# A fourth seven-product pair in every second group of the last stage's first matrix

## The chip, the cores and the metric

The kernel runs on one core of a Trainium2 chip. Its engines are TensorE (PE in the profile, with PEld for the loading of its stationary operand), VectorE (DVE), ScalarE (ACT), GpSimd (POOL) and SyncE (SP), which issues the transfers. Each engine works through its own queue in order and waits on semaphores of the others. The metric is the device time of one execution in microseconds (us). Each measurement is a median over runs; lower is better.

## The reference, cut to what matters

A decoder trunk of two layers on 256 tokens of width 2048. Layer 0 mixes tokens by retention, layer 1 by a gated convolution; each layer ends in a SwiGLU feed-forward part with 5632 hidden columns. The change lies in the feed-forward part of layer 1, the last stage:

```python
D_MODEL, SEQ, DEPTH = 2048, 256, 2
D_FF = -(-8 * D_MODEL // (3 * 256)) * 256     # 5632

def swiglu(h, w_in, w_out):
    a, b = jnp.split(h @ w_in, 2, axis=-1)
    return (jax.nn.silu(a) * b) @ w_out
...
        h = (rms_norm(x, norm2_g[i]) * (1.0 + sc2) + sh2).astype(x.dtype)
        x = (x + g2 * swiglu(h, ffn_w_in[i], ffn_w_out[i])).astype(x.dtype)
    return rms_norm(x, final_g).astype(x.dtype)
```

`w_in` (2048 x 11264) is the first matrix of the stage, `w_out` (5632 x 2048) the second.

## The kernel before

**Arithmetic.** Every float32 operand is split into a high part (the value rounded to the matmul's input type) and a low part (the rest). A product is three matmuls: high by high, high by low and low by high (`thrice`, L470 to L475). ACT casts the high part of the weights (L408), DVE subtracts it from the weights to get the low part (L411). All weights come from memory in 1 MB blocks of 128 x 2048 (`raw`, three buffers), on SP's queue, in the order of their use.

**Weight places.** The prepared high and low parts lie in rings of six places of 1024 columns each (`PLACES`, L403 to L415). PE takes the places in order (`take`); a place can be written again when PE has used it up.

**The last stage.** The hidden columns are handled in two parts, of 20 and 24 tiles of 128 columns. In each part a stretch of first-matrix work is followed by a stretch of second-matrix work. After eight column tiles done in another form (`first_rows`), the first matrix runs in ten groups, 0 to 3 in the first part and 4 to 9 in the second (`LAST_IN`, `last_input`). A group makes four hidden tiles: two blocks of 512 columns (one of `a`, one of `b`) for two halves of 128 tokens, that is four accumulators (`ours`), summed over the 2048 rows of the weights. These rows come as eight *pairs* (0 to 7) of two 128-row tiles; one pair is one 1 MB block. Second-matrix groups have the same form with other pairs.

**An ordinary pair** (`Group`, `by_token`) has two row tiles, two column blocks and two token halves: eight products, 24 matmuls. Its block is prepared as one piece of 2048 columns, in two places.

**A seven** (`Seven`, `sevens`) does the same pair as a 2 x 2 block product with seven products instead of eight (the Strassen-Winograd form), 21 matmuls. It needs sums of the weight blocks and of the activations. The block is prepared in four pieces, four places: (2) the blocks B22 and B21 as they are, (3) two differences T1 and T3 (L395, in a single buffer, which the profile calls `x`), (4) B11 and T2 (L399), (5) T4 (L401), 512 columns wide. PE uses them in the order B22, B21, T1, T3, B11, T2, T4. Four of the products are gathered in four banks of their own over all sevens of a group. After the last seven of the group `mixed_sums` combines them (L1255 to L1259), and when the group is complete the four accumulators are added (L1330), the gate product is made (L1334, L1335), and its tiles are turned by PE at pair 2 of the next group (`turned`, L1344 to L1351). After this the hidden tiles are split on ACT and DVE (L1348, L1349), and for every second one of some groups sums for the second matrix are made (L1156 to L1159, L525).

**The activations' sums.** `made_in_sums` (L1171 to L1183) makes, once, for each pair that is ever a seven, the four sums s1 to s4 of its four activation blocks, and splits each into high and low. Three go to tiles taken from a list of free ones (`single_sums`), the fourth, s3, overwrites the block of `h` that the seven form doesn't use (a21). A pair with s3 in that place cannot be an ordinary pair later. Pairs 3, 4 and 6 are sevens in all ten groups (`IN_SEVEN`, L41).

**Order.** PE's order is written out in the program; on the other engines a scheduler orders the instructions within their data dependences and priorities when the program is built.

Of the kernel before, what the change touches and what calls it, by code (L numbers as in the profile page):

```python
# [11 lines left out]
F32R = mybir.dt.float32r  # L12
# [5 lines left out]
P = 128  # L18
D = 2048
S = 256  # L20
KT = D // P
# [4 lines left out]
DV = 512  # L26
DFF = 5632
# [10 lines left out]
LEAD = 6  # L38
ROOTS_AT, SPREAD_AT = 1, 3
TAIL_ROWS = 6  # L40
IN_SEVEN, OUT_SEVEN, TURNS_AT, BESIDE_CB, BESIDE_SUMS = (3, 4, 6), ((2, 4, 6), (2, 4, 6)), 2, 40, 48  # L41
LAST_TILES = 20, 24
STORE_AT, LOAD_AT = 0, 2
LEAD_RET, LEAD_CONV, LEAD_FFN = 6, 4, 2
# [97 lines left out]
class Seven:  # L142
# [6 lines left out]
    n = 2 * DV // P  # L149
# [12 lines left out]
def in_pairs(cols, rows, sevens):  # L162

    return [Seven(cols, r) if i in sevens else Group(cols, DV, ks=r) for i, r in rows]


def last_in():

    n, rows = LAST_TILES[0], [(i, [2 * i, 2 * i + 1]) for i in range(KT // 2)]
    cols = [part * DFF + j * P for j in range(n - 4, n) for part in range(2)]
    firsts = [Group(cols[:LEAD])] + [Group([c]) for c in cols[LEAD:]]
    fours = [[*range(0, n - 4, 4)], [*range(n, FT, 4)]]
    return firsts, [[in_pairs([j * P, DFF + j * P], rows, IN_SEVEN) for j in js] for js in fours]


def last_out(part):
# [78 lines left out]
def trunk(ctx: ExitStack, tc: tile.TileContext, x_in, c_in, pos_in, w_mod, cols_in, gain_in, tab_in, w_all, out):  # L257
    nc = tc.nc
    const = ctx.enter_context(tc.tile_pool(name="const", bufs=1))
# [10 lines left out]
    def tmp(tag, shape=(P, S), dtype=F32, pool=work, bufs=None):  # L270
        return pool.tile(list(shape), dtype, tag=tag, name=name(tag), bufs=bufs)
# [10 lines left out]
    n_cols = cols_in.shape[1]  # L282
    cols = const.tile([P, n_cols], F32, tag="cols", name="cols")
# [74 lines left out]
    groups = [g for _, _, g in in_use_order()]  # L358
# [3 lines left out]
    in_seven, n = set(), 0  # L362
# [114 lines left out]
    def half_of(h, t):  # L477
        return [h[:, i, t * P : (t + 1) * P] for i in range(2)]
# [127 lines left out]
    h = rows_at(EARLIER)  # L606
# [85 lines left out]
    with ExitStack() as inner:  # L692
# [372 lines left out]
        h = rows_at(0)  # L1065

    mixing = ctx.enter_context(ExitStack())
    mpool = mixing.enter_context(tc.tile_pool(name="mpool", bufs=1))
# [28 lines left out]
    for i, g in enumerate(CONV_IN):  # L1097
        pending += [sums(g)] if i else normed(acc, 1, 0, g)
        while len(pending) >= 3:
            pb, pc, pu = pending[:3]  # L1100
            pending = pending[3:]
            j = done
# [17 lines left out]
    mpool = ctx.enter_context(tc.tile_pool(name="last", bufs=1))  # L1120
# [3 lines left out]
    h = rows_at(EARLIER)  # L1124
# [25 lines left out]
    single_sums = [in_cb[:, n * P : (n + 2) * P].rearrange("p (i n) -> p i n", i=2) for n in (12, 14)]  # L1150

    def tokens_sums_of(a11, a21, a12, a22, third, others):

        u = tmp("u512", (P, DV), pool=mpool, bufs=3)
        s1, s2, s4, s3 = [u[:, n * P : (n + 1) * P] for n in range(4)]
        nc.vector.tensor_tensor(s3, a11, a21, op=ALU.subtract)  # L1156
        nc.vector.tensor_tensor(s1, a21, a22, op=ALU.add)
        nc.vector.tensor_tensor(s2, s1, a11, op=ALU.subtract)
        nc.vector.tensor_tensor(s4, a12, s2, op=ALU.subtract)  # L1159
        split(third, s3)  # L1160
        n = 3 * P // len(others)
        for i, dst in enumerate(others):
            split(dst, u[:, i * n : (i + 1) * n])

    def parts(both):

        return [both[:, i, t * P : (t + 1) * P] for i in range(2) for t in range(2)]

    in_sums = {}

    def made_in_sums():  # L1171

        tmp("beside_sums", (P, BESIDE_SUMS), bufs=1)
        for tag, n in (("u", 3), ("low", 2), ("sum", 4)):
            single_sums.extend(tmp(tag, (P, 2, P), F32R, bufs=n) for _ in range(n))
        for i in IN_SEVEN:
            both = tmp("u512", (P, 2, S), pool=mpool, bufs=3)
            for n in range(2):
                k = 2 * i + n
                high, low = [h[k].bitcast(F32)[:, v, :] for v in range(2)]  # L1180
                nc.vector.tensor_tensor(both[:, n, :], high, low, op=ALU.add)
            in_sums[i] = [single_sums.pop() for _ in range(3)]
            tokens_sums_of(*parts(both), h[2 * i][:, :, P:], in_sums[i])  # L1183

    def three(v):
        return [v[0][:, :, n * P : (n + 1) * P] for n in range(3)] if len(v) == 1 else v
# [8 lines left out]
    def gate_stored():  # L1195
        needed(1, GT2)
        pt = bank()
        nc.tensor.transpose(pt[:KT, 0, :P], mod_g[1][1], ident)
        row = tmp("row", (KT, P), pool=mpool, bufs=1)
        nc.scalar.copy(row, pt[:KT, 0, :P])  # L1200
        nc.sync.dma_start(gate_row, row)

# [33 lines left out]

    def sevens(g, act, base, sums, ours, banks, first, last):

        s1, s2, s4 = [[v[:, n, :] for n in range(2)] for v in sums]
        (a11, s3), (a12, a22) = [[half_of(act[k - base], t) for t in range(2)] for k in g.ks]  # L1240
        p1, p5, p6, p7 = [(b, first, last) for b in banks]
        for use, x, (o, a, z) in zip(g.uses(), (s4, a12, s1, s3, a11, s2, a22), (
            (ours[0, 1], False, False), (ours[0, 0], False, False), p5, p7, p1, p6, (ours[1, 0], False, False)
        )):
            thrice(o, x, take(*use), a, z)
            if use[2] in ("B21", "T3", "T2"):
                paced(4)
        paced(4)
# [33 lines left out]
    def gathered(groups, act, base, sums, beside=None, mixed=None):  # L1282

        ours = {(t, j): flat_bank() for t in range(2) for j in range(2)}
        banks, n = [], len(sums)
        for i, g in enumerate(groups):
            if beside:
                beside(i)
            if i == TURNS_AT and waiting:
                waiting.pop(0)()  # L1290
            if isinstance(g, Seven):
                n -= 1
                banks = banks or [flat_bank() for _ in range(4)]
                of = sums[(g.ks[0] - base) // 2]
                sevens(g, act, base, of, ours, banks, n == len(sums) - 1, n == 0)
                if not n:
                    extra = mixed_sums(banks)
                    if mixed:
                        mixed(extra)
                continue  # L1300
            if len(g.cols) == 1:
                tail = TAIL_ROWS if g is groups[-1] else 0
                late, j = [], g.cols[0] // DV % 2
                for k in g.ks:
                    weights = take(g, k, *g.items[0])
                    rows = (act[k - base], False, k == g.ks[-1])
                    if tail:
                        late.append((*weights, *rows))
                    else:
                        by_token([ours[t, j] for t in range(2)], *weights, *rows)  # L1310
                    paced(g.n)
                for t in range(2):
                    for args in late:
                        by_token([ours[t, j] for t in range(2)], *args, halves=[t])
                    added(t, g.cols[0] // DV, ours[t, j], True)
                    if tail:
                        stored(t)
                continue
            for k in g.ks:
                for j, item in enumerate(g.items):  # L1320
                    ends = i == 0 and k == g.ks[0], g is groups[-1] and k == g.ks[-1]
                    by_token([ours[t, j] for t in range(2)], *take(g, k, *item), act[k - base], *ends)
                paced(g.n)
        return ours, extra

    def last_input(groups, pairs, seven):

        ours, extra = gathered(groups, h, 0, in_sums)
        for (t, j), pt in ours.items():
            nc.vector.tensor_tensor(extra[t, j], pt, extra[t, j], op=ALU.add)  # L1330
        ms = []
        for t in range(2):
            m = extra[t, 0]
            nc.scalar.activation(m, m, AF.Silu)  # L1334
            nc.vector.tensor_tensor(m, m, extra[t, 1], op=ALU.mult)  # L1335
            ms.append(m)

        def turned():
            for n, (dst, of) in enumerate(zip(pairs, seven)):
                pt = bank()  # L1340
                for i in range(2):
                    for t, m in enumerate(ms):
                        c = slice((2 * n + i) * P, (2 * n + i + 1) * P)
                        nc.tensor.transpose(pt[:, i, t * P : (t + 1) * P], m[:, c], ident)  # L1344
                if of is not None:
                    both = tmp("u512", (P, 2, S), pool=mpool, bufs=3)
                    nc.scalar.copy(both, pt)
                nc.scalar.copy(dst[:, :, 0, :], pt)  # L1348
                nc.vector.tensor_tensor(dst[:, :, 1, :], pt, dst[:, :, 0, :].bitcast(F32), op=ALU.subtract)  # L1349
                if of is not None:  # L1350
                    tokens_sums_of(*parts(both), dst[:, 0, :, P:], of)  # L1351

        waiting.append(turned)
# [47 lines left out]
    for part in range(2):  # L1401
        n = LAST_TILES[part] // 2
# [48 lines left out]
```

## Time and profile before

| | us |
|---|---|
| median of 3 runs | 2594.94 (2594.69 to 2596.77) |
| the profiled execution, its own time | 2595.16 |
| its span, first to last instruction | 2593.4 |
| groups 0 to 3 (first matrix, first part) on PE | 1925.45 to 2094.43 |
| groups 4 to 9 (first matrix, second part) on PE | 2201.28 to 2454.69 |

In the profile, L is a line of the kernel. A timeline row has the start, the duration, the engine, the line, the operation, output and input tiles with their sizes, and the number of instructions merged in the row; in brackets stands how long the engine was idle before, and who released it. Rows of one engine overlap a little, because an instruction starts before the one ahead of it has drained: what an instruction costs a busy engine is the distance between starts. A windows row has the stretch, its length, then for PE, PEld, DVE, ACT and POOL the busy time with the number of instructions, the granted clock of TensorE, the share of the DMA engines and GB/s.

### The profile page before, as it was taken

The numbers are of one execution on the slowest core, as the hardware profiler recorded it, in microseconds if no ns is written. First come the engines' busy times: TensorE is split into PE (matmuls) and PEld (weight loads), VectorE is DVE, ScalarE is ACT, GpSimd is POOL, SyncE is SP. The second block draws the span as 40 slices with busy tenths as digits, with TensorE's granted clock in tenths as the row PEclk, the third lists the DMA queues.
The fourth block names the chain that finished last, engine by engine and source line by source line (L and its number), as shares of the span: only waits on it lengthen the run. The fifth ranks groups of instructions, "written<-read, shape, count | busy, mean of one in ns | idle before, by whom it ended". The sixth has DMA issues, their size and how long they took to land.

```text
span 2593.4 us, 35836 instructions
## 1 busy us (share of the span) xinstructions
PE 2560.4 (99%) x14181; PEld 2236.5 (86%) x14181; DVE 2167.7 (84%) x2378; ACT 1301.9 (50%) x1792; POOL 158.3 (6%) x232
## 2 busy tenths in 40 slices
PE   7999999999999999999999999999999999999998
PEld 6898889888889888888888898888998888888886
DVE  7988878787698887777777889988988988999877
ACT  5544543444456444334454454444565554555554
POOL 0000000200000000111101200000000000000002
PEclk9999999999999999999999999999999999999999
DMA  9975768767676888778777768887845465455553
GB/s 398 386 309 199 275 239 302 296 260 276 245 284 248 314 335 312 278 306 303 291 299 291 288 248 302 329 304 281 307 155 220 179 234 204 177 213 188 218 200 142
DMA packets 96684, 689.53 MB, mean 266 GB/s; under 512 B 10737, under 2 KB 12161, under 8 KB 13441
## 3 DMA queue, kind: packets, MB, share of 16 engines
q1 hardware_dynamic: 96514, 687.23, 70.4%
q8 instruction: 111, 1.82, 0.3%
q14 instruction: 59, 0.48, 0.1%
HBM read 685.08 MB, written 2.11 MB: 265 GB/s over the span
## 4 chain that ended last, share of the span: by engine, by line
PE 93%; DVE 3%; issue 2%; DMA 1%; ACT 1%; ACTq 0%; POOLq 0%; POOL 0%; DVEq 0%
PE bank L460 29%; PE bank L463 15%; PE bank L473 12%; PE bank L474 12%; PE bank L475 12%; PE bank L509 2%; PE bank L508 2%; PE bank L507 2%; PE bank L640 1%; PE bank L642 1%; PE bank L641 1%; DVE lo L411 1%; DVE raw L768 1%; DMA raw<-w_all 1%; PE bank L996 1%
## 5 line engine op out<-in xcount | busy, mean ns | idle before, releaser
L408 ACT CAST hi<-raw 128x1024 fp32r<-128x1024 f32 (+1 forms) x954 | 968.2, 1032 | 900.2 <-DMA raw<-w_all 344.7
L411 DVE TENSOR_TENSOR lo<-raw,hi 128x2048 fp32r<-128x2048 f32 (+2 forms) x570 | 1078.8, 1901 | 257.8 <-ACT hi L408 256.2
L460 PE MATMUL bank<-h,hi 128*128 128x512 f32 x2016 | 699.2, 390 | 0.0
L463 PE MATMUL bank<-h,lo 128*128 128x256 f32 x2016 | 568.4, 282 | 0.0
L460 PEld LDWEIGHTS bank<-h,hi 128*128 128x128 f32 x2016 | 378.3, 188 | 79.2
L318 DVE SCALAR_TENSOR_TENSOR raw<-raw,cb 128x2048 f32<-128x2048 f32 x160 | 365.9, 2287 | 75.8 <-DMA raw<-w_mod 75.8
L473 PE MATMUL bank<-hi,h 128*128 128x512 f32 x1032 | 404.4, 392 | 2.5 <-DVE rm L752 2.5
L474 PE MATMUL bank<-lo,h 128*128 128x512 f32 x1032 | 402.9, 390 | 0.0
L475 PE MATMUL bank<-hi,h 128*128 128x512 f32 x1032 | 402.1, 390 | 0.0
L463 PEld LDWEIGHTS bank<-h,lo 128*128 128x128 f32 x2016 | 381.0, 189 | 0.0
L460 PE MATMUL bank<-mid,hi 128*128 128x512 f32 x922 | 319.8, 390 | 0.0
L463 PE MATMUL bank<-mid,lo 128*128 128x256 f32 x922 | 260.0, 282 | 0.0
L473 PEld LDWEIGHTS bank<-hi,h 128*128 128x128 f32 x1032 | 194.3, 188 | 40.8 <-DVE rm L752 3.2
L475 PEld LDWEIGHTS bank<-hi,h 128*128 128x128 f32 x1032 | 194.0, 188 | 41.0
L474 PEld LDWEIGHTS bank<-lo,h 128*128 128x128 f32 x1032 | 194.2, 188 | 37.5 <-DVE lo L411 0.3
L460 PEld LDWEIGHTS bank<-mid,hi 128*128 128x128 f32 x922 | 173.0, 188 | 36.3
L463 PEld LDWEIGHTS bank<-mid,lo 128*128 128x128 f32 x922 | 174.3, 189 | 0.0
L460 PE MATMUL bank<-rm,hi 128*128 128x512 f32 x496 | 172.5, 390 | 0.0
L509 PE MATMUL bank<-h,lo 128*128 128x256 f32 x512 | 146.7, 286 | 5.5 <-DVE lo L411 5.5
L507 PE MATMUL bank<-h,hi 128*128 128x256 f32 x512 | 146.2, 286 | 3.5 <-ACT h L796 3.5
L508 PE MATMUL bank<-h,hi 128*128 128x256 f32 x512 | 146.1, 285 | 0.7 <-DVE h L797 0.7
L463 PE MATMUL bank<-rm,lo 128*128 128x256 f32 x496 | 139.8, 282 | 0.0
(256 smaller groups left out, 3230.3 us busy)
## 6 DMA issues: line engine op xcount, KB each, us to landing
raw<-w_all SPq DMA_DIRECT2D x456, 1024.0 KB, 4.9
raw<-w_mod SPq DMA_DIRECT2D x192, 1024.0 KB, 5.1
x<-x_in SPq DMA_DIRECT2D x4, 512.0 KB, 5.4
out<-xt SPq DMA_DIRECT2D x4, 512.0 KB, 3.0
decay<-tab_in SPq DMA_DIRECT2D x8, 128.0 KB, 3.4
x<-gate_row SPq DMA_DIRECT2D x2, 512.0 KB, 4.4
last_gain<-gain_in SPq DMA_DIRECT2D x1, 1024.0 KB
cols<-cols_in SPq DMA_DIRECT2D x1, 152.0 KB, 8.9
```

The costliest lines, as they stand in the source:

```text
L318: nc.vector.scalar_tensor_tensor(raw, raw, 1.0, cb, op0=ALU.mult, op1=ALU.mult, accum_out=total)
L408: nc.scalar.copy(hi[:, o], raw[:, o])
L411: nc.vector.tensor_tensor(lo, raw, hi.bitcast(F32), op=ALU.subtract)
L460: nc.tensor.matmul(pt, hi, h, start=fresh and k == g.ks[0], stop=False, skip_group_check=True)
L463: nc.tensor.matmul(pt[:, 1, :], lo, h[:, 0, :], start=False, stop=last and k == g.ks[-1], skip_group_check=True)
L473: nc.tensor.matmul(o, hi, w_hi, start=first, stop=False)
L474: nc.tensor.matmul(o, hi, w_lo, start=False, stop=False)
L475: nc.tensor.matmul(o, lo, w_hi, start=False, stop=last)
L507: nc.tensor.matmul(pt, hi, h[:, 0, :], start=first, stop=False, skip_group_check=True)
L508: nc.tensor.matmul(pt, hi, h[:, 1, :], start=False, stop=False, skip_group_check=True)
L509: nc.tensor.matmul(pt, lo, h[:, 0, :], start=False, stop=last, skip_group_check=True)
L640: nc.tensor.matmul(pt, hi, high, start=k == 0, stop=False, skip_group_check=True)
```

## The change

In groups 0, 2, 4, 6 and 8 of the ten, pair 5 is a seven as well: these groups have the sevens 3, 4, 5 and 6 in a row, the others 3, 4 and 6 as before. Because pair 5 stays an ordinary pair in the other groups, its block a21 of `h` has to stay, and s3 of pair 5 gets a tile of its own (`third`). With its other three sums that makes four tiles; the list of free ones is longer by one, which lies over the tile of the modulation's columns (`cols`), and it is taken from the end, so the sums of the other pairs move by one tile. The tile for the gate's row (`row`) is no longer one of its own, but one of the three `u512` buffers.

```diff
-IN_SEVEN, OUT_SEVEN, TURNS_AT, BESIDE_CB, BESIDE_SUMS = (3, 4, 6), ((2, 4, 6), (2, 4, 6)), 2, 40, 48
+IN_SEVENS, OUT_SEVEN, TURNS_AT, BESIDE_CB, BESIDE_SUMS = ((3, 4, 5, 6), (3, 4, 6)), ((2, 4, 6), (2, 4, 6)), 2, 40, 48
...
     fours = [[*range(0, n - 4, 4)], [*range(n, FT, 4)]]
-    return firsts, [[in_pairs([j * P, DFF + j * P], rows, IN_SEVEN) for j in js] for js in fours]
+    sevens = {j: IN_SEVENS[i % 2] for i, j in enumerate(sum(fours, []))}
+    return firsts, [[in_pairs([j * P, DFF + j * P], rows, sevens[j]) for j in js] for js in fours]
...
-        for i in IN_SEVEN:
+        single_sums.append(const.tile([P, n_cols], F32R, tag="cols", name="in_cols")[:, : 2 * P].rearrange(
+            "p (i n) -> p i n", i=2
+        ))
+        for i in IN_SEVENS[0]:
...
-            tokens_sums_of(*parts(both), h[2 * i][:, :, P:], in_sums[i])
+            third = h[2 * i][:, :, P:]
+            if i not in IN_SEVENS[1]:
+                third = mpool.tile([P, 2, P], F32R, tag="third", name="third")
+                in_sums[i].append(third)
+            tokens_sums_of(*parts(both), third, in_sums[i][:3])
...
-        row = tmp("row", (KT, P), pool=mpool, bufs=1)
+        row = tmp("u512", (P, DV), pool=mpool, bufs=3)[:KT, :P]
...
-        s1, s2, s4 = [[v[:, n, :] for n in range(2)] for v in sums]
+        s1, s2, s4, *third = [[v[:, n, :] for n in range(2)] for v in sums]
         (a11, s3), (a12, a22) = [[half_of(act[k - base], t) for t in range(2)] for k in g.ks]
+        s3 = third[0] if third else s3
...
-        ours, extra = gathered(groups, h, 0, in_sums)
+        used = [g.ks[0] // 2 for g in groups if isinstance(g, Seven)]
+        ours, extra = gathered(groups, h, 0, {i: in_sums[i] for i in used})
```

## The prediction

> **What bounds the kernel now.** I read the page first.
>
> ```profile
> span 2593.4 us, 35836 instructions
> PE 2560.4 (99%) x14181; PEld 2236.5 (86%) x14181; DVE 2167.7 (84%) x2378; ACT 1301.9 (50%) x1792; POOL 158.3 (6%) x232
> PE 93%; DVE 3%; issue 2%; DMA 1%; ACT 1%; ACTq 0%; POOLq 0%; POOL 0%; DVEq 0%
> ```
>
> PE is busy 99% of the span and is 93% of the chain that ended last, so work taken from PE shortens the kernel wherever the others keep up. DVE's 84% is an average; the windows view, cut at the boundaries of the groups that change (in order 0, 2, 4, 6, 8) and, second, of one that does not, says how it stands where the change is.
>
> ```profile
> 1925.45:1967.24 41.79, 41.79 (x187) 34.36 (x185) 39.38 (x59) 25.43 (x40) 0.00 (x0) 1.00 0.53 197
> 1967.24:2009.62 42.38, 42.38 (x192) 35.17 (x191) 38.08 (x39) 24.09 (x27) 0.00 (x0) 1.00 0.54 199
> 2009.62:2052.01 42.39, 42.39 (x192) 35.17 (x191) 39.26 (x45) 25.24 (x30) 0.00 (x0) 1.00 0.55 198
> 2201.28:2242.76 41.48, 41.48 (x185) 34.35 (x183) 37.73 (x39) 21.95 (x23) 0.00 (x0) 1.00 0.54 197
> 2285.15:2327.53 42.38, 42.38 (x192) 35.17 (x191) 39.42 (x45) 25.22 (x30) 0.00 (x0) 1.00 0.53 197
> 2369.92:2412.31 42.39, 42.39 (x193) 35.17 (x192) 39.25 (x45) 25.18 (x30) 0.00 (x0) 1.00 0.53 200
> ```
>
> After the length come PE, PEld, DVE, ACT and POOL, each with its count. PE never waits for long, at full granted clock (1.00), but in group 2 DVE has only 42.39 - 39.26 = 3.13 us left. What a seven costs each engine decides.
>
> **PE's gain.** Ordinary pairs take 24 matmuls and a seven 21, so each of the five groups loses three. The price is the distance of starts, not the duration. Here are the first matmuls of pairs 4 and 5 of group 2; pair 4 is a seven.
>
> ```profile
> 2031.61 0.39 PE L473 MATMUL bank<-hi,low 128*128 128x512 f32 x1
> 2036.37 0.39 PE L473 MATMUL bank<-hi,h 128*128 128x512 f32 x1
> ```
>
> 21 matmuls in 4.76 us are 0.2267 us each. 3 x 0.2267 = 0.68 us a group, 3.4 us in all: 0.13% of the time if nothing else moves. By the duration that the rows show (0.39 us each) it would be 15 x 0.39 = 5.85 us. The Trainium skill's "Perfetto Trace Analysis" (Identifying the Most-Contended Engine) says matmul busy share is a poor measure because matmuls are pipelined; the two starts above bear that out, 0.23 apart against 0.39 long.
>
> **DVE's cost of a seven.** DVE rows of group 2, from the turned tiles of the group before to the end of pair 4. The order of the changed program is the same up to the last row, which there begins pair 5.
>
> ```profile
> 2013.88 2.29 DVE L411 TENSOR_TENSOR lo<-raw,hi 128x2048 fp32r<-128x2048 f32 x1
> 2016.08 1.22 DVE L395 TENSOR_TENSOR x<-raw 128x1024 f32<-128x1024 f32 x1
> ...
> 2022.25 0.69 DVE L1349 TENSOR_TENSOR mid<-bank,mid 128x512 fp32r<-128x512 f32 x1 [0.34 <-ACT mid L1348]
> ...
> 2025.07 1.22 DVE L395 TENSOR_TENSOR x<-raw 128x1024 f32<-128x1024 f32 x1
> 2026.20 0.55 DVE L525 TENSOR_TENSOR in_cb<-u,in_cb 128x384 fp32r<-128x384 f32 x1
> 2026.67 1.22 DVE L411 TENSOR_TENSOR lo<-raw,hi 128x1024 fp32r<-128x1024 f32 x1
> 2027.81 0.68 DVE L399 TENSOR_TENSOR raw<-raw,x 128x512 f32<-128x512 f32 x1
> 2028.41 1.22 DVE L411 TENSOR_TENSOR lo<-x,hi 128x1024 fp32r<-128x1024 f32 x1
> 2029.55 0.68 DVE L401 TENSOR_TENSOR raw<-raw 128x512 f32<-128x512 f32 x1
> 2030.15 1.82 DVE L411 TENSOR_TENSOR lo<-raw,hi 128x1024 fp32r<-128x1024 f32 x2
> 2031.88 1.22 DVE L395 TENSOR_TENSOR x<-raw 128x1024 f32<-128x1024 f32 x1
> ```
>
> An ordinary pair is one 2048-wide subtraction, start to start 2016.08 - 2013.88 = 2.20 us. A seven is seven DVE instructions, 2031.88 - 2025.07 = 6.81 us less the 0.47 of L525 between them: 6.34 us. Start to start, a 1024-wide one is 1.14, a 512-wide one 0.60. So pair 5 adds 4.14 us to DVE and takes 0.68 from PE. In groups 2, 6 and 8 DVE's work becomes about 39.3 + 4.1 = 43.4 us against 42.39 - 0.68 = 41.7 for PE. Worse, pairs 3 to 6 stand in one block, where DVE needs 6.34 a pair and PE 4.76, and the six places of prepared halves hold one and a half sevens (four places each): DVE cannot build up a lead in the groups between, and L1349 above waits for ACT's copy of what PE turns at pair 2 of the same group, so DVE cannot run ahead of that point. What is late next is pair 6, its last piece, and pair 7.
>
> Walk of group 2, in the changed program's DVE order: from 2031.88, pair 5 6.34 (2038.22); pair 6 without its last 512 piece 5.74 (2043.96); then the scheduler puts pair 7's 2.20 ahead (2046.16), and pair 6's last piece runs 0.69, ready at 2046.85. PE starts pair 5 at 2036.37, pair 6 at 2041.13, its seventh product 18 x 0.2267 = 4.08 later, and the low half is used by the second matmul: 2045.44. How such lateness looks, and what it costs beyond, group 0 shows already (pair 5's subtraction, then its first three matmuls):
>
> ```profile
> 1949.36 3.42 DVE L411 TENSOR_TENSOR lo<-raw,hi 128x2048 fp32r<-128x2048 f32 x2
> 1951.40 0.39 PE L473 MATMUL bank<-hi,h 128*128 128x512 f32 x1
> 1951.69 0.50 PE L474 MATMUL bank<-lo,h 128*128 128x512 f32 x1
> 1952.03 0.39 PE L475 MATMUL bank<-hi,h 128*128 128x512 f32 x1
> ```
>
> The subtraction ends at 1949.36 + 2.29 = 1951.65, PE goes on 0.04 later, and the next start is 0.34 instead of 0.23 away: 0.11 extra. So group 2 waits 2046.89 - 2045.44 = 1.45, plus 0.11, less 0.68: **+0.9 us**. The rows for groups 6 and 8, DVE's first after pair 4 and PE's first of pair 5, and for group 4:
>
> ```profile
> 2307.41 1.22 DVE L395 TENSOR_TENSOR x<-raw 128x1024 f32<-128x1024 f32 x1
> 2311.89 0.39 PE L473 MATMUL bank<-hi,h 128*128 128x512 f32 x1
> 2392.18 1.22 DVE L395 TENSOR_TENSOR x<-raw 128x1024 f32<-128x1024 f32 x1
> 2396.66 0.39 PE L473 MATMUL bank<-hi,h 128*128 128x512 f32 x1
> 2223.07 0.68 DVE L399 TENSOR_TENSOR raw<-raw,x 128x512 f32<-128x512 f32 x1
> 2227.12 0.39 PE L473 MATMUL bank<-hi,h 128*128 128x512 f32 x1
> ```
>
> Groups 6 and 8 have group 2's order, and DVE is as far ahead (2311.89 - 2307.41 and 2396.66 - 2392.18, both 4.48; group 2 4.49): +0.9 each. In the changed order of group 4 pair 5's difference (1.14) is already made at 2223.07. What is left before pair 6's third piece, 1024 wide, is 6.34 - 1.14 = 5.20 of pair 5, 6.34 - 1.14 - 0.60 = 4.60 of pair 6, and pair 7's 2.20, which again stands ahead: it begins at 2235.07 and is ready 1.22 later, 2236.29. PE wants it 4.76 + 12 x 0.2267 + 0.23 = 7.71 after 2227.12, at 2234.83. 1.46 + 0.04 + 0.11 - 0.68: **+0.9**.
>
> **Group 0 pays more**, because row 5's own sums are made right before it (2 additions of 256, 4 of 128, 4 splits of 128).
>
> ```profile
> 1930.15 0.75 DVE L1181 TENSOR_TENSOR u<-h 128x256 f32<-128x256 f32 x2
> 1930.82 0.28 DVE L1156 TENSOR_TENSOR u<-u 128x128 f32<-128x128 f32 x1
> 1931.02 0.28 DVE L1157 TENSOR_TENSOR u<-u 128x128 f32<-128x128 f32 x1
> 1961.80 0.39 PE L473 MATMUL bank<-hi,h 128*128 128x512 f32 x1
> ```
>
> 0.67 + 8 x 0.20 = 2.27 us on DVE. From 1930.15 it then has three such sets (6.81) and four sevens (25.36) before pair 7: 1962.32, and 2.29 + 0.04 until PE may use it, 1964.65. Pair 7 can start 0.23 before that, 1964.42; the last row is its start now, 1961.80. The stalls lie at pairs 5, 6 and 7. +2.6, 0.1 for the restarts: **+2.7**.
>
> **What costs nothing.** ACT gets two more casts a group (four for a seven, two for an ordinary pair) and four small ones once: at 25.2 of 42.4 us it has the room, and its casts for pairs 5 and 6 fit between DVE's steps. If they did not, that is the third rival. The weights are the same 1 MB loads in the same order on SP's queue. The new tile over the columns waits for POOL's last read of them; POOL is idle in all windows above. The gate's row now holds one of three u512 tiles:
>
> ```profile
> gate_row<-row SPq DMA_DIRECT2D x1, 8.0 KB, 3.4
> 2094.71 0.26 ACT L1200 COPY row<-bank 16x128 f32<-16x128 f32 x1 [1.01 <-PE bank L1198]
> 2106.65 0.58 ACT L1347 COPY u<-bank 128x512 f32<-128x512 f32 x1
> ```
>
> The copy ends at 2094.97, its store lands about 3.4 us later, and the next u512 is written at 2106.65: 8 us of cover. Without it the wait would be below 3.4.
>
> **The sum.** 2.7 + 4 x 0.9 = +6.3 us on the profiled execution's own 2595.16: 2601.5. That execution lies 0.22 above the median of 2594.94, so the forecast for the median is **2601.3**, slower by 0.25%. Own range: 2598 to 2604.
>
> **The rivals.**
> *The places cover four groups.* If in groups 2, 4, 6 and 8 the last late piece comes before PE wants it, each gives its 0.68, and group 0's +2.7 cancels them: 2595. For it: DVE idles in these groups (3.13 us in group 2). Against: that idle time falls where the places are full, outside the block. It decides if DVE stands 1.45 us earlier at the end of pair 4, 2030.4 instead of 2031.88. One mechanism, the other side: not slower. 0.20.
> *DVE is never late*: 2591.5, all 3.4. It needs the walk of group 0 wrong by 3 us too. 0.05.
> *The hand-over between ACT and DVE shows.*
>
> ```profile
> 1946.47 1.82 DVE L411 TENSOR_TENSOR lo<-raw,hi 128x1024 fp32r<-128x1024 f32 x2 [0.47 <-ACT hi L408]
> ```
>
> A piece must be cast before its low half is made, and DVE idles 0.47 us here for that, at the end of pair 4 of group 0. In pairs 5 and 6 of five groups it would be 10 x 0.47 = 4.7 more: 2606.0. Against: in the changed order another instruction mostly stands between. 0.13.
>
> *The duration is the price and DVE hides*: 2589.1, faster. 0.02. The rest, 0.02, lies outside.
>
> **How the numbers follow.** The forecast has 0.58. About 0.2% (5.2 us) is what a measurement of this kernel can tell from no change. The line is at 2600.1, inside the forecast's own range: of its 0.58 I give 0.11 to below it. Same: 0.11 + 0.20 + 0.05 = 0.36; faster 0.03; slower 0.61. The range reaches from just below the first rival to the third, 2594.4 to 2606.4.
>
> **What would show it.** Right: PE gaps of 1 to 2 us, ended by the low half (L411's successor), late in pair 6 of groups 2, 4, 6 and 8, and from pair 5 on in group 0; DVE without idle time from pair 3 to pair 7; the groups between as long as now (42.4). Wrong: changed groups of 41.7 us, DVE idle inside the block, or stalls in the groups between.

## The result, and the profile after

The changed kernel takes 2601.61 us (median of 8 runs, 2599.6 to 2605.45) against 2592.82 us (8 runs, 2592.2 to 2596.77) for the kernel before on the same chip: the ratio is 1.0032, 95% interval 1.0021 to 1.0043, or some 8 us slower (5 to 11). The profiled execution took 2601.1 us.

Its page first: the span, the engines (busy time, share of the span, instructions) and the chain that ended last.

```profile
span 2599.3 us, 35852 instructions
PE 2560.9 (99%) x14166; PEld 2232.5 (86%) x14166; DVE 2191.1 (84%) x2418; ACT 1311.9 (50%) x1806; POOL 153.7 (6%) x232
PE 90%; DVE 4%; DMA 2%; issue 2%; ACT 1%; ACTq 0%; POOLq 0%; POOL 0%; DVEq 0%
```

The counts are those of the edit: PE 15 fewer (five groups, three each), DVE 40 more (five times six, and ten for row 5's sums), ACT 14 more (five times two, and four). PE's busy time still did not fall, in part because a matmul that waits for its operand, or that runs at a lower clock, is recorded longer (0.50 and 0.69 us in the rows below, against 0.39).

The windows view, cut where PE starts a group: groups 0, 1, 2, 3 and 4 (columns as in the prediction: length; PE, PEld, DVE, ACT, POOL with counts; clock, DMA share, GB/s).

```profile
1922.77:1968.09 45.32, 42.79 (x184) 33.41 (x182) 44.77 (x77) 27.90 (x47) 0.00 (x0) 1.00 0.44 168
1968.09:2010.54 42.45, 42.45 (x192) 35.17 (x191) 38.59 (x38) 24.21 (x27) 0.00 (x0) 1.00 0.57 213
2010.54:2053.86 43.32, 42.16 (x189) 34.45 (x188) 42.77 (x53) 25.39 (x31) 0.00 (x0) 1.00 0.47 173
2053.86:2096.34 42.48, 42.48 (x193) 35.10 (x192) 39.63 (x43) 26.18 (x32) 0.00 (x0) 1.00 0.58 219
2203.22:2247.95 44.73, 42.80 (x182) 34.85 (x180) 42.37 (x47) 23.07 (x26) 0.00 (x0) 0.96 0.49 185
```

Against the rows of before, group 0 is 3.53 us longer (45.32 - 41.79), group 2 0.93 (43.32 - 42.39; groups 6 and 8 the same), group 4 3.25 (44.73 - 41.48), and the groups in between, which the change leaves alone, about 0.07 (42.45 - 42.38). DVE has 0.55 us left in group 2, where it had 3.13, and PE stands still for 43.32 - 42.16 = 1.16.

PE's rows show where: before the twentieth of pair 6's 21 matmuls in groups 2, 6 and 8, before the fourteenth in group 4 (start, duration, engine, line, operation; in brackets the idle time before and what ended it). Group 2:

```profile
2046.29 0.39 PE L474 MATMUL bank<-hi,h 128*128 128x512 f32 x1
2047.84 0.50 PE L475 MATMUL bank<-lo,h 128*128 128x512 f32 x1 [1.16 <-DVE lo L412]
```

and group 4:

```profile
2236.64 0.39 PE L474 MATMUL bank<-hi,h 128*128 128x512 f32 x1
2238.95 0.69 PE L475 MATMUL bank<-lo,h 128*128 128x512 f32 x1 [1.93 <-DVE lo L412]
2239.44 0.63 PE L476 MATMUL bank<-hi,h 128*128 128x512 f32 x1
...
2242.00 0.63 PE L476 MATMUL bank<-hi,h 128*128 128x512 f32 x1
```

Each wait is for a low half that DVE makes in L412. In group 2 the starts are 2047.84 - 2046.29 = 1.55 us apart, 1.32 more than the usual 0.23; in group 4 2.31, 2.08 more, and after that matmuls start 0.43 apart instead of 0.23 for about 3.4 us (from 2239.44 to 2242.00 there are six such steps). DVE's rows for group 2, from pair 6 on:

```profile
2039.15 1.22 DVE L396 TENSOR_TENSOR x<-raw 128x1024 f32<-128x1024 f32 x1
...
2043.16 0.68 DVE L402 TENSOR_TENSOR raw<-raw 128x512 f32<-128x512 f32 x1
2043.76 6.23 DVE L412 TENSOR_TENSOR lo<-raw,hi 128x1024 fp32r<-128x1024 f32 x4
```

No row has an idle time, those left out neither. The last one stands for four subtractions: pair 6's third piece, pair 7's 2048 columns, pair 6's last 512 and the next group's first 2048 (1.14 + 2.20 + 0.60 + 2.29 = 6.23).

Group 0 has five such waits, here without the third and fourth:

```profile
1949.69 0.50 PE L475 MATMUL bank<-lo,u 128*128 128x512 f32 x1 [0.27 <-DVE lo L412]
1952.57 0.49 PE L475 MATMUL bank<-lo,low 128*128 128x512 f32 x1 [1.22 <-DVE lo L412]
...
1962.70 0.50 PE L475 MATMUL bank<-lo,h 128*128 128x512 f32 x1 [0.20 <-DVE lo L412]
```

They lie in pairs 5, 6 and 7, and with the two left out (0.45 and 0.39) add up to 2.53 us of idle time.

### The profile page after: what moved, and what is told of

It reads as the page before. It is cut to its first block, busy times and chain, and to the rows that moved or that the text cites. A ratio compares the mean times of both kernels' runs of the same rounds, so it can differ in the third digit from the quotient of the medians.

```text
span 2599.3 us, 35852 instructions
## 1 busy us (share of the span) xinstructions
PE 2560.9 (99%) x14166; PEld 2232.5 (86%) x14166; DVE 2191.1 (84%) x2418; ACT 1311.9 (50%) x1806; POOL 153.7 (6%) x232
## 4 chain that ended last, share of the span: by engine, by line
PE 90%; DVE 4%; DMA 2%; issue 2%; ACT 1%; ACTq 0%; POOLq 0%; POOL 0%; DVEq 0%
PE bank L461 29%; PE bank L464 15%; PE bank L475 11%; PE bank L474 11%; PE bank L476 11%; PE bank L509 2%; PE bank L510 2%; PE bank L508 2%; DVE lo L412 2%; DMA raw<-w_all 1%; PE bank L641 1%; PE bank L643 1%; PE bank L642 1%; ACT hi L409 1%; DVE raw L769 1%
## 5 line engine op out<-in xcount | busy, mean ns | idle before, releaser
L412 DVE TENSOR_TENSOR lo<-raw,hi 128x2048 fp32r<-128x2048 f32 (+2 forms) x580 | 1082.6, 1876 | 250.9 <-ACT hi L409 249.7
L475 PE MATMUL bank<-lo,h 128*128 128x512 f32 x1007 | 394.4, 392 | 6.1 <-DVE lo L412 6.1
L474 PE MATMUL bank<-hi,h 128*128 128x512 f32 x1007 | 395.1, 392 | 1.8 <-DVE rm L753 1.8
L476 PE MATMUL bank<-hi,h 128*128 128x512 f32 x1007 | 392.9, 390 | 0.0
L474 PEld LDWEIGHTS bank<-hi,h 128*128 128x128 f32 x1007 | 189.8, 189 | 39.6 <-DVE rm L753 2.4
L476 PEld LDWEIGHTS bank<-hi,h 128*128 128x128 f32 x1007 | 189.4, 188 | 40.0
```

The lines of the kernel that those rows point to most:

```text
L412: nc.vector.tensor_tensor(lo, raw, hi.bitcast(F32), op=ALU.subtract)
L474: nc.tensor.matmul(o, hi, w_hi, start=first, stop=False)
L475: nc.tensor.matmul(o, hi, w_lo, start=False, stop=False)
L476: nc.tensor.matmul(o, lo, w_hi, start=False, stop=last)
```

## The experiments

The lengths in the tables are from PE's first matmul of a group to that of the next, as in the windows above. Where an expectation speaks of 2.96 us for group 0, it counts from other boundaries; from PE's first matmul on it is 3.53.

| kernel | time, us | ratio to before | 0 | 1 | 2 | 3 | 4 | 6 | 8 |
|---|---|---|---|---|---|---|---|---|---|
| before | 2592.6 to 2593.1 | 1 | 41.79 | 42.38 | 42.39 | 42.42 | 41.48 | 42.38 | 42.39 |
| the change | 2601.61 | 1.0032 | 45.32 | 42.45 | 43.32 | 42.48 | 44.73* | 43.32 | 43.31 |
| the change again | 2600.47 | 1.0030 [1.0017, 1.0042] | 45.31 | 42.46 | 43.32 | 42.48 | 43.13 | 43.31 | 43.32 |
| sums alone | 2594.33 | 1.0006 [0.9997, 1.0015] | 43.53 | 42.46 | 42.45 | 42.48 | 41.54 | 42.45 | 42.46 |
| DVE spared | 2589.23 | 0.9985 [0.9976, 0.9994] | 41.20 | 42.46 | 41.80 | 42.56 | 40.90 | 41.81 | 41.81 |
| pair 7 in two | 2599.48 | 1.0025 [1.0015, 1.0035] | 45.70 | 42.46 | 42.25 | 43.76 | 42.81 | 42.26 | 42.25 |
| late sums | 2598.19 | 1.0020 [1.0011, 1.0028] | 41.80 | 43.01 | 42.98 | 42.51 | 44.72* | 43.32 | 43.32 |
| other order | 2600.87 | 1.0031 [1.0020, 1.0043] | 41.81 | 43.01 | 44.32 | 42.52 | 40.90 | 45.97* | 44.31 |
| tiles moved | 2600.58 | 1.0028 [1.0017, 1.0039] | 45.28 | 42.39 | 43.32 | 42.41 | 44.72* | 43.37 | 43.37 |
| POOL, late sums | 2602.48 | 1.0038 [1.0024, 1.0052] | 41.81 | 43.01 | 44.93 | 42.59 | 43.45 | 44.92 | 44.93 |
| POOL, early sums | 2609.44 | 1.0064 [1.0052, 1.0077] | 48.62* | 42.39 | 44.95 | 42.54 | 43.71 | 44.92 | 44.92 |

A star marks a group in which TensorE ran at half clock for 3.4 us of this profile (below). Groups 5, 7 and 9 stay within 0.13 us of before in all of them, but for group 7 with pair 7 in two (43.77).

### The change once more

No edit: the changed kernel itself, on the chip of the next three.

> The changed kernel once more, without an edit. If DVE's lateness is the cause, its gaps on PE repeat to a few hundredths: one of 1.55 us near the end of pair 6 in groups 2, 6 and 8, of more than 2 us in group 4, four of 0.6 to 1.6 us in group 0, and the kernel is again 0.2 to 0.4% slower than before. What is open is the half clock after the gap of group 4 (matmuls 0.43 us apart instead of 0.23, some 1.6 us in all): if any gap over 2 us brings it, it is there again; if it hangs on the moment at which the gap falls, it can be missing or stand behind another gap, and the time moves by one or two us with it.

Every wait came back at its place and to 0.04 us of its size, with one exception: the half clock behind group 4's wait did not. The windows of the changed kernel's first profile, cut at 2239.09 and 2242.51, where the granted clock changes, with the stretch of the same length ahead:

```profile
2235.68:2239.09 3.41, 1.48 (x7) 0.90 (x7) 3.41 (x3) 3.12 (x4) 0.00 (x0) 1.00 0.12 24
2239.09:2242.51 3.42, 3.42 (x9) 2.65 (x10) 3.38 (x4) 0.59 (x1) 0.00 (x0) 0.50 0.96 335
```

and of the second, where the wait ends 1.9 us later, two stretches of that length that share the wait:

```profile
2236.60:2240.02 3.42, 2.32 (x11) 1.57 (x9) 3.12 (x3) 3.42 (x5) 0.00 (x0) 1.00 0.29 120
2240.02:2243.43 3.41, 2.59 (x11) 2.18 (x12) 3.41 (x3) 1.24 (x2) 0.00 (x0) 1.00 0.69 267
```

The granted clock fell to 0.50 in the first and stayed at 1.00 in the second. So of group 4's 3.25 us in the first profile 44.73 - 43.13 = 1.60 is the clock, and 1.65 is the wait with what the group saves.

### The sums alone

Row 5's sums are made as in the change, and no group uses them.

```diff
-    sevens = {j: IN_SEVENS[i % 2] for i, j in enumerate(sum(fours, []))}
+    sevens = {j: IN_SEVENS[1] for j in sum(fours, [])}
```

> Row 5's sums are made, but no group has a fourth seven. DVE theory: only group 0 pays, because 2.27 us of DVE work stand before its first seven, and it was late there by 0.17 already: group 0 is 43.9 us instead of 41.8, the others 42.4, and the kernel is about 2 us (0.1%) slower than before. Rival, that the sums' new tiles slow PE: every group longer by the same amount, about 0.06 us, 0.6 in all, with nothing in group 0 that the others don't have.

Group 0 is 1.74 us longer (43.53 - 41.79), with one wait in front of pair 5:

```profile
1922.42:1965.95 43.53, 42.19 (x186) 34.28 (x185) 41.54 (x70) 26.80 (x44) 0.00 (x0) 1.00 0.50 188
1950.41 0.50 PE L475 MATMUL bank<-lo,h 128*128 128x512 f32 x1 [1.34 <-DVE lo L412]
```

So the sums made alone cost half of what group 0 pays. That is not a fixed price: the late piece here is pair 5's 2048-wide subtraction (from 1948.07), with pair 6's difference (1946.93) ahead of it on DVE, and in the next experiment group 0 makes the same sums and does not wait. All other groups are 0.06 to 0.08 us longer although they have three sevens as before; that is taken up below.

### DVE spared

The fourth seven stays on PE, but DVE makes for it only what an ordinary pair costs, 2048 columns of low halves: the differences and the low halves of the last two pieces are left out, so that pair 5 multiplies other numbers there.

```diff
-        if piece == 2:
+        if piece == 2 and not short_of:
             nc.vector.tensor_tensor(differences, whole[:, DV : 3 * DV], whole[:, : 2 * DV], op=ALU.subtract)
...
-        nc.vector.tensor_tensor(lo, raw, hi.bitcast(F32), op=ALU.subtract)
+        if not (short_of and piece in (4, 5)):
+            nc.vector.tensor_tensor(lo, raw, hi.bitcast(F32), op=ALU.subtract)
```

> The fourth seven stays with its 21 matmuls, its four pieces and four places, but DVE makes for it what it makes for an ordinary pair, 2048 columns of low halves; the differences and the low halves of its last two pieces are left out, so its products are of other numbers. DVE theory: groups 2, 4, 6 and 8 get PE's gain and no gap, 41.75 us (group 4 40.85); group 0 pays for the sums, about 1.5 us; the kernel is 1 to 2 us faster than before. Rival, that the fourth seven is slow on PE or by its places (four instead of two): the gaps stay, 43.3 us a group, +6 us or more.

All waits are gone, and each changed group is 0.57 to 0.59 us shorter than before, group 0 too, which was expected to pay some 1.5 us for the sums: with pair 5 in pieces of 1024 columns DVE begins its first low half at 1947.29, PE does not wait, and the sums cost nothing. Groups 2 and 4:

```profile
2006.45:2048.25 41.80, 41.80 (x189) 34.61 (x188) 38.84 (x47) 26.35 (x32) 0.00 (x0) 1.00 0.52 192
2197.68:2238.58 40.90, 40.90 (x182) 33.78 (x180) 37.40 (x41) 22.96 (x25) 0.00 (x0) 1.00 0.50 193
```

PE is busy for the whole length of both. ACT's casts, the weights' loads and the new tiles are all still there, so DVE's work on the fourth seven is the cause of the waits. (ACT's casts of the differences no longer wait for DVE here either; in group 2 of the change that hand-over cannot be the cause, since DVE has no idle time from pair 4 to pair 7.) PE's gain is real: 0.68 less some 0.1, most of which the moved tiles below explain.

### Pair 7 in two

In the changed groups pair 7 is prepared as two pieces of 1024 instead of one of 2048, so that only 1.14 us of it can stand ahead of pair 6's last piece.

```diff
+            if g.ks == [10, 11] and g.cols[1] - g.cols[0] == DFF:
+                after_seven.add(n // CHUNK + 2)
...
-        for p in ((2, 3, 4, 5) if i in in_seven else (0, 1) if i < halved else (6,))
+        for p in ((2, 3, 4, 5) if i in in_seven else (0, 1) if i < halved or i in after_seven else (6,))
```

> Pair 7 of the five groups is prepared in two pieces of 1024 columns instead of one of 2048, so that on DVE only 1.14 us instead of 2.20 stand ahead of the late piece of pair 6; DVE's work is the same. Theory that the order on DVE makes the gap: the gap of groups 2, 6 and 8 shrinks from 1.55 to about 0.5 us and the group from 43.3 to 42.2; group 4's from 2.3 to about 1.2, and no half clock behind it; group 0 about as long as now; the kernel 3 to 6 us faster than the changed one. Rival, that the sum of DVE's work (43.4 us in a group) sets its length: the gap moves to pair 7 and the groups stay at 43.3.

Groups 2, 6 and 8 did lose 1.07 us of their wait (0.48 between the starts instead of 1.55), but groups 3 and 7 then wait, in pairs 4 and 5. Groups 2 and 3, and group 3's two waits:

```profile
2011.73:2053.98 42.25, 42.16 (x189) 34.46 (x188) 41.88 (x53) 24.68 (x31) 0.00 (x0) 1.00 0.47 171
2053.98:2097.74 43.76, 43.07 (x193) 34.94 (x192) 40.53 (x44) 26.47 (x32) 0.00 (x0) 1.00 0.58 220
2079.36 0.50 PE L477 MATMUL bank<-lo,h 128*128 128x512 f32 x1 [0.22 <-DVE lo L414]
2082.17 0.50 PE L477 MATMUL bank<-lo,h 128*128 128x512 f32 x1 [0.47 <-DVE lo L414]
```

The two together last 86.01 us, against 43.32 + 42.48 = 85.80 in the change. The 2048-wide piece in front decides where PE waits. What DVE is behind, it can be behind in the next group if PE doesn't wait for it in this one. It need not be: groups 1, 5 and 9, for which DVE has 37 or 38 instructions against the 44 of groups 3 and 7, do not wait.

### The sums made later

Group 0 keeps three sevens, and row 5's sums are made during group 1; groups 2, 4, 6 and 8 are as in the change.

```diff
-    sevens = {j: IN_SEVENS[i % 2] for i, j in enumerate(sum(fours, []))}
+    sevens = {j: IN_SEVENS[i % 2 or i == 0] for i, j in enumerate(sum(fours, []))}
...
-            made_in_sums()
+            made_in_sums(IN_SEVENS[1])
         for i, groups in enumerate(LAST_IN[part]):
+            if i == 1 and not part:
+                made_in_sums((5,))
```

> Group 0 keeps three sevens; row 5's own sums are made during group 1, and groups 2, 4, 6 and 8 keep the fourth seven. Theory (each group pays for itself: what DVE cannot finish inside the block of pairs 3 to 6): group 0 back to 41.8 to 41.9 us between its starts on PE, group 1 stays at 42.45 although it takes the 2.27 us of sums (DVE has 4.3 us left there), groups 2, 6 and 8 unchanged at 43.3, group 4 43.1 (44.7 if the half clock comes again). Time about 2597.5 against 2593.1 before and 2600.5 for the change. Rival (the lateness is handed on from group 0): groups 2 to 8 get shorter too, to 42.4 or less, and the time goes to 2594 or below. Other rival: the sums are as dear in group 1 as in group 0: group 1 longer by 2 us, time 2599.5.

Groups 1 and 2:

```profile
1965.88:2008.89 43.01, 42.74 (x192) 35.10 (x191) 40.28 (x50) 24.87 (x31) 0.00 (x0) 1.00 0.55 196
2008.89:2051.87 42.98, 42.19 (x190) 34.46 (x188) 42.59 (x52) 26.12 (x32) 0.00 (x0) 1.00 0.51 184
```

Group 0 is back at its length of before, and groups 4, 6 and 8 are as long as in the change (group 2 is 0.34 shorter, behind group 1's wait): each pays for itself. The hope that group 1 would hide the sums failed in part, with 0.6 us there (43.01 against 42.45), although DVE is busy for only 40.28 us of it. Room in a group is no room in the block of sevens.

### Another order of the pairs

As the late sums, with the pairs in the order 0, 1, 3, 4, 2, 5, 6, 7 in groups 2, 4, 6 and 8: two sevens, an ordinary pair, two sevens.

```diff
+    mixed_up = [rows[i] for i in (0, 1, 3, 4, 2, 5, 6, 7)]
-    return firsts, [[in_pairs([j * P, DFF + j * P], rows, sevens[j]) for j in js] for js in fours]
+    return firsts, [
+        [in_pairs([j * P, DFF + j * P], mixed_up if 5 in sevens[j] else rows, sevens[j]) for j in js] for js in fours
+    ]
```

> The kernel with the late sums, and in groups 2, 4, 6 and 8 the eight pairs of rows are taken in the order 0, 1, 3, 4, 2, 5, 6, 7, so that never more than two sevens stand together. DVE's work and PE's work are the same to the instruction, only their order differs. Theory (the block of four is what costs: DVE falls 1.58 us behind per seven and can lead by no more than its six places): two sevens cost 3.2 us of lead, which an ordinary pair between them gives back (4.76 + 0.68 - 2.20 = 3.2), as in the kernel before; no stall, groups 2, 6 and 8 at 41.8, group 4 at 40.9; time 2590 to 2591, below the kernel before. Rival (the sum of DVE's work in the group, 43.4 us, sets it, wherever the sevens stand): groups 2, 6 and 8 at 43.3 as now, or stalls in the groups after them; time about 2597.5, as with the late sums alone.

The theory held in group 4 alone, which has no wait left and is 0.58 us shorter than before. The other three became longer. Groups 2 and 4, then group 2's wait:

```profile
2009.35:2053.67 44.32, 42.17 (x190) 34.54 (x188) 43.31 (x51) 26.13 (x32) 0.00 (x0) 1.00 0.48 184
2203.08:2243.98 40.90, 40.90 (x181) 33.78 (x180) 39.82 (x43) 23.53 (x25) 0.00 (x0) 1.00 0.53 199
2031.28 0.50 PE L478 MATMUL bank<-lo,h 128*128 128x512 f32 x1 [2.15 <-DVE lo L415]
```

The wait is now in the fourth pair, the second seven, where the starts are 2.53 us apart. DVE's rows ahead of it:

```profile
2012.54 0.69 DVE L1349 TENSOR_TENSOR x<-bank,x 128x512 f32<-128x512 f32 x1
...
2027.81 4.02 DVE L415 TENSOR_TENSOR lo<-raw,hi 128x2048 fp32r<-128x2048 f32 x3
```

Before it can go on with the first seven, DVE finishes the group before (L1349, L1354: 2012.54 to 2016.13, 3.59 us), and it makes the turned tiles 6.5 us later. Directly ahead of the piece that PE waits for stands again a 2048-wide subtraction, that of the ordinary pair 2: the last row is that one (2.20 us), the second seven's third piece (ready at 2027.81 + 2.20 + 1.22 = 2031.23, PE goes on at 2031.28) and its last. In group 4, the first behind an output stage, there are no tiles to turn (DVE has work of that stage in between instead), and the second seven's last two pieces (2216.67) come before the 2048-wide subtraction (2220.75). So the rows name two things ahead of the late piece, the work of the group before and the 2048-wide subtraction; no run took either away alone.

### The two tiles moved

The changed kernel, with the sums' tile over the columns and the third sum read 96 and 64 bytes further on, at multiples of 128 bytes.

```diff
-        single_sums.append(const.tile([P, n_cols], F32R, tag="cols", name="in_cols")[:, : 2 * P].rearrange(
+        single_sums.append(const.tile([P, n_cols], F32R, tag="cols", name="in_cols")[:, 24 : 24 + 2 * P].rearrange(
...
-                third = mpool.tile([P, 2, P], F32R, tag="third", name="third")
+                third = mpool.tile([P, 16 + 2 * P], F32R, tag="third", name="third")
+                third = third[:, 16:].rearrange("p (i n) -> p i n", i=2)
```

> The changed kernel, only that the two new tiles of sums which stand at 32 and 64 bytes past a multiple of 128 (the one over the columns and the third sum) are read 96 and 64 bytes further on, at a multiple of 128 as the other sums' tiles are. Theory (the place of the stationary operand's tile makes the matmuls that use it 390 to 399 ns instead of 389): all of them 389 ns, groups 1, 3, 5, 7 and 9 at 42.38 to 42.40 instead of 42.45, groups 2, 6 and 8 unchanged or 0.1 less, since there the wait for DVE sets the end; time 0.3 to 0.6 us less than the change, which the comparison cannot tell. Rival (something else makes pair 3 longer, the order of its weights for one): 394, 399 and 390 ns as now, 42.45.

The matmuls on the tile over the columns, by line (count, then ns: lowest, median, highest; first and last start), in the change

```profile
L474 PE MATMUL bank<-hi,in_cols x10: 394/394/394, 1940.6 to 2438.1; 128*128 128x512 f32 x10
L475 PE MATMUL bank<-lo,in_cols x10: 399/399/399, 1940.8 to 2438.3; 128*128 128x512 f32 x10
L476 PE MATMUL bank<-hi,in_cols x10: 390/390/390, 1941.0 to 2438.6; 128*128 128x512 f32 x10
```

and here, with group 1:

```profile
L475 PE MATMUL bank<-lo,in_cols x10: 389/389/389, 1941.0 to 2438.3; 128*128 128x512 f32 x10
1968.25:2010.64 42.39, 42.39 (x193) 35.17 (x191) 38.61 (x38) 24.49 (x27) 0.00 (x0) 1.00 0.60 214
```

So the 0.07 us of the untouched groups (group 1: 42.45 in the change, 42.39 here) is the place of that tile. For the third sum the theory did not hold: its three matmuls took 404, 395 and 397 ns (medians) here against 398, 393 and 397, and what makes them longer is open. Both moves together with the other order gave 2601.55 us (1.0030, 1.0019 to 1.0042):

> The order 0, 1, 3, 4, 2, 5, 6, 7 with late sums, and the two tiles moved to multiples of 128. By both theories: groups 2, 6 and 8 at 41.7, the groups between at 42.4, no matmul of a seven above 389 ns but after waits; time 2589.5 to 2590.5. By the rival of the order: 2597.

Its groups show what the two show apart: group 1 43.03, 2 44.33, 4 40.84, 6 44.42, 8 45.94 (with the half clock), 5 and 9 42.39.

### The differences on POOL

POOL makes the fourth seven's three differences. The first kernel has the late sums, and the tile over the columns moved as above.

```diff
+        less = nc.gpsimd if block in by_pool else nc.vector
...
-            nc.vector.tensor_tensor(differences, whole[:, DV : 3 * DV], whole[:, : 2 * DV], op=ALU.subtract)
+            less.tensor_tensor(differences, whole[:, DV : 3 * DV], whole[:, : 2 * DV], op=ALU.subtract)
```

(and so for the two of 512 columns)

> The kernel with the late sums, the tile over the columns read at a multiple of 128 bytes, and the three subtractions of the fourth seven's differences (one of 1024, two of 512) made by POOL instead of DVE, in groups 2, 4, 6 and 8. Theory (it is DVE's work inside the block of pairs 3 to 6 that is late): the fourth seven costs DVE 6.34 - 1.14 - 2 x 0.60 = 4.00 us, less than PE's 4.76 for the pair before it, so the lead does not fall further; groups 2, 6 and 8 at 41.8 us instead of 43.3, group 4 at 40.9, no gap in pair 6; group 1 keeps its 43.0 with row 5's sums; time 2590.5 to 2591.5, below the kernel before. Rival (POOL is slower than DVE for such a subtraction, or slows DVE down beside it): DVE's 1024-wide subtractions longer than 1.22 us while POOL runs, or a wait for POOL in front of ACT's casts of pair 5; gaps of 1 to 3 us in pair 5 or 6, time 2597 or more.

The second has the early sums and four sevens in group 0 again, with row 5's sums and differences on POOL too.

> As pool_diff, with group 0 a group of four sevens again and row 5's sums made ahead of it as in the change, but their sums and differences by POOL (only the 256-wide halves' splits stay with DVE). Theory: group 0 loses most of its 2.96 us, since DVE saves 2.34 us of the seven and 2 x 0.34 + 4 x 0.20 of the sums: between 41.1 and 42 us; the other groups as in pool_diff, group 1 at 42.4; time 2589.5 to 2590.5, some 3 us below the kernel before. Rival: POOL's additions stand in front of its subtractions and come late for pair 3 or 5 of group 0: group 0 at 43 to 45 as now, time 2592 to 2594.

The first is 4.3 us slower than the late sums alone, the second 8 us slower than the change. POOL's groups of the first kernel (line, engine, operation, count, busy us, mean ns, idle before):

```profile
L399 POOL TENSOR_TENSOR x<-raw 128x1024 f32<-128x1024 f32 x4 | 16.0, 3992 | 489.6 <-DVE lo L415 489.6
L403 POOL TENSOR_TENSOR raw<-raw,x 128x512 f32<-128x512 f32 x4 | 8.6, 2158 | 0.3
```

and, in group 2, POOL's first and DVE's rows beside its three:

```profile
2030.38 4.52 POOL L399 TENSOR_TENSOR x<-raw 128x1024 f32<-128x1024 f32 x1 [148.50 <-DVE lo L415]
2030.82 1.83 DVE L415 TENSOR_TENSOR lo<-raw,hi 128x1024 fp32r<-128x1024 f32 x2
2032.90 3.10 DVE L415 TENSOR_TENSOR lo<-raw,hi 128x1024 fp32r<-128x1024 f32 x1 [0.25 <-ACT hi L412]
2036.03 2.20 DVE L415 TENSOR_TENSOR lo<-x,hi 128x1024 fp32r<-128x1024 f32 x1
```

POOL's rows are longer than DVE's 1.22 and 0.68 us: 4.52 us for 1024 columns in three groups and 2.40 in group 4, about 2.15 for 512. Part of that is waiting for DVE (last section). Beside them DVE's own 1024-wide subtraction takes 3.10 and 2.20 us. Of the 2.34 us that DVE should have saved, 3.10 + 2.20 - 2 x 1.22 = 2.86 are gone at once. That is the rival as it was written, both halves of it.

## Why the prediction was right, and where it was short

**Who is late, and where.** Right. DVE's fourth seven is the cause (DVE spared: no wait left), and the waits stand where the walk put them: late in pair 6 of groups 2, 4, 6 and 8, from pair 5 on in group 0.

**PE's gain.** 0.68 us a group was right: 0.57 to 0.59 measured with DVE spared, and most of the rest is the 0.06 or so of the tile over the columns, which the prediction did not have. The duration as the price (1.17 us a group) is ruled out.

**Groups 2, 6 and 8.** +0.9 each predicted, +0.93 measured. Waiting cost 1.52 us (43.32 against 41.80 with DVE spared) where the walk had 1.45 + 0.11 = 1.56.

**Group 4.** +0.9 predicted, +1.65 measured without the half clock and +3.25 with it. The walk made DVE's block from distances of starts as they are when another instruction stands in between. In group 4 the scheduler puts the three that depend on one another in a row:

```profile
2232.63 1.22 DVE L412 TENSOR_TENSOR lo<-x,hi 128x1024 fp32r<-128x1024 f32 x1
2233.76 0.69 DVE L400 TENSOR_TENSOR raw<-raw,x 128x512 f32<-128x512 f32 x1
2234.48 0.69 DVE L402 TENSOR_TENSOR raw<-raw 128x512 f32<-128x512 f32 x1
2235.47 6.23 DVE L412 TENSOR_TENSOR lo<-raw,hi 128x2048 fp32r<-128x2048 f32 x4 [0.30 <-ACT hi L409]
```

L402 starts 0.72 after L400 instead of 0.60, and the next 0.99 after that, with 0.30 of idle time for ACT's cast: 0.12 + 0.39, and 0.12 once more in pair 5 (2227.29 to 2228.01). That is 0.63, and the wait was 2.08 instead of 1.46 + 0.04, longer by 0.58. In part this is the third rival, the hand-over between ACT and DVE: 0.30 of idle time where it named 0.47 a seven; the sign "DVE without idle time from pair 3 to pair 7" held in group 2 from pair 4 on, not here. Where the low halves stand in between, as in group 2, it does not show, as the prediction said.

**Group 0.** +2.7 predicted, +3.53 measured. The sums made alone cost 1.74. DVE's three sets and four sevens took 35.1 us up to the end of pair 7's subtraction (1927.47 to 1962.56) where the walk had 6.81 + 25.36 + 2.20 = 34.4; most of the 0.7 is again in longer steps between dependent instructions, as in group 4 (1955.90 to 1956.62 to 1957.48 for two that take 0.60 each when mixed with others; 0.17 of it is idle time for ACT's cast).

**The groups between.** "As long as now" was wrong by 0.07 us each: not DVE, but the place of a tile.

**The sum.** +6.3 predicted. The second profile's ten groups add up to 3.52 + 0.93 + 1.65 + 0.92 + 0.94 for the changed ones and 0.35 for the others, 8.3 us; the ratios of the times say 8.3 in the first comparison and 7.8 in the second. That the forecast of 2601.3 us came so close to 2601.61 is luck: the sum was 2 us too small, and the kernel before ran 2 us faster in this comparison than in the runs that the forecast starts from. The step that was mis-sized is the price of DVE's block in groups 0 and 4, too small by 0.83 and 0.75 us, most of it through the steps between dependent instructions; a half clock, which adds 1.6 us when it comes, was not in any term.

**What costs nothing.** Right for ACT's room, the loads and the gate's row: with DVE spared PE never waits in these groups, and the first output group, where the row is stored, takes 54.52 us against 54.49.

**The first rival** (the places cover four groups): what would have let it be true is 1.45 us of lead. Pair 7 in two gave 1.07 of it, and behind groups 2 and 6 the lateness went into the next group. The late sums and the other order say the same from other sides: what DVE has free lies where the places are full. None of the kernels that compute everything was faster than the kernel before.

## What to carry to other kernels

An operation that saves time on the engine that is the bound, and costs more on the one that feeds it, is priced in the block where it stands, not in the mean of a group or of the kernel: here 0.68 us of PE against 4.14 of DVE, with 3.1 us of DVE free in the group, cost 0.9. Price a chain of small dependent instructions from rows in which they stand next to each other, since they start later (0.72 apart, and 0.99 with 0.30 of it idle for a cast) than the same ones mixed with others (0.60). Moving the late piece or the order shifts the wait; before giving work to an idle engine, look whether it slows the busy one.

## What the runs showed of the hardware

**The half clock after a wait.** In the ten groups of the change and of the experiments PE's starts lie 2.3 to 2.8 us apart eleven times; after six of them TensorE runs at a granted clock of 0.50 for 3.41 us, with matmuls 0.43 apart, which costs about 1.6 us. After the other five, and after every wait of 2.0 us or less in these groups, the clock stayed at 1.00. It is not the length alone that decides: the wait of 2.3 us in group 4 of the changed kernel brought it in one profile and not in the other. What differs is where the wait lies on a grid. Each of the six begins a whole number of 3.4133 us after the trace's first record of the clock (in the change 23.84 + 649 x 3.4133 = 2239.09). With the time cut on this grid, PE was busy for only 1.09 to 1.50 us of the 3.41 ahead of each of the six. In the other five the wait lay across a border of the grid, as in the second profile above, and the emptiest stretch still had 1.78. How little work brings the half clock is not settled by this: at about 125 us, in an earlier stage, it came once after 1.88 us and once did not after 1.58. The Trainium skill's "TensorE: Matmul & The Clock Gate" (Part 1: The HAM clock gate) has a free-running window of about 3.4 us, after which an idle array gets half the clock. The grid agrees with that; but the windows that bring it here were not idle, PE worked in them for up to 1.5 us.

**POOL and DVE.** DVE's 1.22 us became 3.10 and 2.20 beside POOL's subtractions, and POOL's own 1024 columns took from 2.40 to 4.52 us. The rows fit two engines that wait for each other's whole instruction, though POOL's spans are rough. In group 2 DVE works without a pause until 2030.82 + 1.83 = 2032.65; POOL's row, begun at 2030.38, ends at 2034.90, 2.25 us after that. In group 4 POOL begins when DVE has just run dry, and needs 2.40:

```profile
2223.62 2.40 POOL L399 TENSOR_TENSOR x<-raw 128x1024 f32<-128x1024 f32 x1 [184.25 <-DVE lo L415]
```

DVE's 3.10 in group 2 ends at 2036.00, 1.10 after POOL's end, and 1.14 is what such a subtraction costs. So POOL's own work on 1024 columns is some 2.3 us, an estimate from these two, twice DVE's and not four times. The Trainium skill's "SBUF — State Buffer" (Who interferes with whom) says that a DVE instruction with two inputs in SBUF contends with one of GpSimd that reads SBUF, and calls the pair of ports that they share an exclusive lock. The rows agree with both.

**The place of a stationary tile.** Where the change has the tile over the columns (by the expectation 32 bytes past a multiple of 128), its matmuls took 394, 399 and 390 ns, and 96 bytes further on 389 each. The third sum's tile, moved by 64 bytes, did not follow.
